# Feed-forward gate and up products of a two-layer trunk: eight half products against Strassen's seven

## The chip, the cores and the metric

One core of a Trainium2 chip runs the whole program. The metric is the device time of one execution in microseconds. Three runs of the kernel before gave 2757.32, 2754.48 and 2758.7 us, a median of 2757.32 us.

## The reference

A trunk of two layers works on 1088 tokens (1024 of a prompt and 64 of a running stream) of width 1024. Layer 0 mixes with a gated convolution and gated linear attention, layer 1 with banded softmax attention. Each layer ends with a SwiGLU feed-forward of inner width 2816:

```python
def swiglu_ffn(h, w_in, w_out):
    gate, up = jnp.split(h @ w_in, 2, axis=-1)
    return (jax.nn.silu(gate) * up) @ w_out
...
x = x + swiglu_ffn(rms_norm(x, norm_ffn[layer]), w_ffn_in[layer], w_ffn_out[layer])
```

Everything is float32, and the results are wanted at about that precision.

## The kernel before

Activations lie transposed: the 1024 features are 8 tiles of 128 partitions (`KT`), the 1088 tokens are the free axis, cut into groups of 384, 384 and 320 (`GROUPS`). To keep precision, each operand is split into a rounded part "hi" and a rest "lo", and each product is three matmuls: hi·hi, hi·lo and lo·hi. The split is a cast on ScalarE (ACT) and a subtraction on VectorE (DVE). `chain` (L241) is one output tile for one token group: 3 matmuls for each of the tiles of the inner axis into one PSUM bank, then an evacuation. `gemm` (L253) is three chains with one weight tile, so 72 matmuls for 8 inner tiles.

Weights come in one list in order of use. `fetch` (L219) issues the DMA of the next one from the queue of SyncE (SP) into the only raw buffer `wraw` and splits it into one of two buffers `whi` and `wlo`. `next_weights` (L236) hands out one weight tile and fetches another, so that one split tile and one on its way are ahead of the matmuls. TensorE (PE) runs in the order of the program text; the order of the other engines and of the SP queue is set by a list scheduler that takes what is ready first by its own model, with priorities; instructions within an engine's queue, once placed, start in that order. `order` (L41) is a planner that spreads side work (norms, attention units) between the matmuls.

The feed-forward (`ffn`, L720) walks the 22 inner tiles in three parts (8, 7 and 7, `FPARTS` L27). For each inner tile it runs a gate gemm and an up gemm over all 8 feature tiles (L740, L741). The gate evacuation multiplies by the reciprocal norm `RS` (L730) and applies SiLU on ACT; the up evacuation multiplies by `RS` (L736), by the gate (L737) and splits the result (L271). After each part `out_gemm` (L716) multiplies the part's tiles with the second weight matrix, eight output tiles, and adds each chain to the residual `X` (L705), which lies in SBUF for the whole feed-forward. In the last part of layer 0 the evacuation also makes the next layer's split input (L266, L267), its sum of squares (POOL, L279) and a store to DRAM (L758); in layer 1 it stores the result (L1164).

The output projection ahead of the feed-forward of layer 1 (L1156 to L1163) starts with 18 short chains of two inner tiles.

Of the kernel before, what the change touches and what calls it, by code (L numbers as in the profile page):

```python
# [131 lines left out]
def trunk_kernel(  # L132
# [6 lines left out]
    act, dve, pe, sp = nc.scalar, nc.vector, nc.tensor, nc.sync  # L139
    order = PEOrder()  # L140
# [6 lines left out]
    apool = ctx.enter_context(tc.tile_pool(name="apool", bufs=1))  # L147
# [17 lines left out]
    RS = [const.tile([P, c1 - c0], F32, name=f"rs{i}") for i, (c0, c1) in enumerate(GROUPS)]  # L165
# [24 lines left out]
    def mm_tile():  # L190
        return cur["ps"].tile([P, 512], F32, name="mm")

    def mm(out, lhsT, rhs, start, stop):
        pe.matmul(out, lhsT, rhs, start=start, stop=stop)  # L194
        n = rhs.free_size()
        order.spend(max(214.0, n / 0.6) if lhsT.dtype == F32 else max(107.0, n / 2.4))
# [3 lines left out]
        order.spend(107.0)  # L200


    wlist = [(w_in[i], KT) for i in range(w_in.shape[0])] + [(w_out[n], KT) for n in range(KT)]
    def ffn_weights(layer):
        for f0, f1 in FPARTS:
            for f in range(f0, f1):
                wlist.append((w_f1[layer, 2 * f], KT))
                wlist.append((w_f1[layer, 2 * f + 1], KT))
# [10 lines left out]
    def fetch():  # L219
        if wpos[0] == len(wlist):  # L220
            return
        src, nk = wlist[wpos[0]]
        wpos[0] += 1
        raw = wpool.tile([P, KT, P], F32, name="wraw", bufs=1)
        sp.dma_start(raw[:, 0:nk, :], src)
# [8 lines left out]
        wready.append((hi, lo))  # L234
# [27 lines left out]
    def scratch():  # L262
        return scratch_r().bitcast(F32)
# [286 lines left out]
    e = dd[1]  # L550
# [169 lines left out]
    def ffn(layer, xgn, aslots, X, after, nxt, g_idx):  # L720
        for pi, (f0, f1) in enumerate(FPARTS):
            acts = []
            for f in range(f0, f1):
                ah, al = aslots[f - f0]
                acts.append((ah, al))
                sbuf_s = {}

                def evac_gate(g, c0, c1, ps):
                    s = scratch()[:, 0:c1 - c0]
                    dve.tensor_tensor(s, ps, RS[g], op=ALU.mult)  # L730
                    silu(s)
                    sbuf_s[g] = s

                def evac_up(g, c0, c1, ps):
                    u = tmp.tile([P, GW], F32, name="ta")[:, 0:c1 - c0]
                    dve.tensor_tensor(u, ps, RS[g], op=ALU.mult)  # L736
                    dve.tensor_tensor(u, u, sbuf_s[g], op=ALU.mult)  # L737
                    split(u, ah[:, c0:c1], al[:, c0:c1])

                gemm(xgn, evac_gate)  # L740
                gemm(xgn, evac_up)  # L741
            last = pi == len(FPARTS) - 1
            if last and nxt is not None:
                log_exp_tables()
            out_gemm(acts, X, after, nxt, last, g_idx)


    mx0.close()
    f0 = ctx.enter_context(ExitStack())
    cur["ps"] = f0.enter_context(tc.tile_pool(name="ps1", bufs=6, space=PSUM))  # L750
    x_sp = dram.tile([KT, P, T], F32, name="x_sp")
    a_sp = dram.tile([KT, P, T], F32, name="a_sp")
    with tc.tile_pool(name="xres", bufs=1, side="right") as xp:
# [398 lines left out]
    X = [bp.tile([P, T], F32, name=f"x1_{n}") for n in range(KT)]
    for g, (c0, c1) in enumerate(GROUPS):
        for n in range(KT):
            sp.dma_start(X[n][:, c0:c1], x_sp[n, :, c0:c1])
    wb = [next_weights() for _ in range(w_ob.shape[0])]  # L1156
    for g in range(len(GROUPS)):
        for n in range(NA):
            ks = slice(n % NB * (KT - KA), (n % NB + 1) * (KT - KA))
            hi, lo = wb[n // NB]  # L1160
            chain((hi[:, ks, :], lo[:, ks, :]), Y1[KA:], g, out_evac(X, n, None, xgf, True, 3))
    for n in range(NA, KT):
        gemm(Y1, out_evac(X, n, None, xgf, True, 3))  # L1163
    ffn(1, xgf, Y1, X, lambda n, c0, c1: sp.dma_start(o_y[n, :, c0:c1], X[n][:, c0:c1]), None, 0)  # L1164
    order.flush()


# [87 lines left out]
```

## Time and profile before

| what | us |
|---|---|
| median of 3 runs | 2757.32 |
| the profiled execution | 2754.32 |
| its span, first to last instruction | 2752.6 |
| PE busy (matmul) in the span | 2683.9 |
| DVE busy | 1309.3 |
| ACT busy | 972.2 |
| POOL busy | 294.8 |

The granted clock of PE is 0.995 of full speed over the span. The two feed-forwards lie at about 483 to 1271 us and 1965 to 2752 us; the attention of layer 1 lies between them, and the mixers of layer 0 ahead. Rows of the profile name an engine, a source line, an operation, the output and the inputs with their shapes, then a count and durations. A duration of a single matmul row overlaps with the next: the pace of PE is the distance from start to start. SPq rows are issues of DMAs by SP.

### The profile page before, as it was taken

To read this page: it belongs to the slowest core of one execution; us is meant where nothing else is said; L and a number is where in the kernel's file an instruction comes from. 1 tells how busy PE (TensorE), PEld (TensorE's weight loads), DVE (VectorE), ACT (ScalarE), POOL (GpSimd) and SP (SyncE) were. 2 spreads that over 40 slices of the span, in tenths; PEclk is the share of its full clock that TensorE was granted. 3 is DMA by queue.
4 is the path that set the end of the run, shared out by engine and by line. 5 is a ranking of instruction groups with operands and counts; after the bars stand their busy time and mean duration, and the time that the engine had idled before them with its cause. 6 is when DMAs were issued, how large, how long until landed. Compare 5 with 4: busy or idle time off the path is not lost.

```text
span 2752.6 us, 40413 instructions
## 1 busy us (share of the span) xinstructions
PE 2683.9 (98%) x16514; PEld 2619.9 (95%) x16514; DVE 1309.3 (48%) x2797; ACT 972.2 (35%) x1950; POOL 294.8 (11%) x361
## 2 busy tenths in 40 slices
PE   8999999999999999999999999989999999999999
PEld 8888999999999999999888888979999999999999
DVE  7545444433233323344778777775633223323332
ACT  5524123321012112234777778865422112211210
POOL 0000002000000000013333333342200000000000
PEclk9999999999999999999999999999999999999999
DMA  5010131111111111122111111143211111111112
GB/s 170 24 34 27 46 105 53 39 47 46 46 47 39 45 48 47 45 79 93 49 57 56 53 55 52 55 136 128 74 39 47 46 46 47 39 47 47 47 54 82
DMA packets 73738, 160.75 MB, mean 58 GB/s; under 512 B 11296, under 2 KB 44592, under 8 KB 73520
## 3 DMA queue, kind: packets, MB, share of 16 engines
q1 hardware_dynamic: 73552, 158.16, 17.9%
q8 instruction: 130, 2.13, 0.3%
q14 instruction: 56, 0.46, 0.1%
HBM read 136.98 MB, written 25.08 MB: 59 GB/s over the span
## 4 chain that ended last, share of the span: by engine, by line
PE 81%; ACT 8%; DVE 7%; issue 2%; DMA 2%; POOL 1%; SPq 0%; DVEq 0%; POOLq 0%; ACTq 0%
PE mm L194 75%; ACT s L932 2%; DVE s L928 1%; PE ao L194 1%; PE pt L199 1%; PE misc L194 1%; PE kv L194 1%; ACT ph L270 1%; ACT s L936 1%; DVE pl L271 1%; PE S L194 1%; ACT whi L229 1%; PE tr L194 1%; DVE s L938 1%; DMA ta<-in_cv_dram 1%
## 5 line engine op out<-in xcount | busy, mean ns | idle before, releaser
L194 PE MATMUL mm<-a,whi 128*128 128x384 f32 (+1 forms) x5760 | 1453.6, 332 | 10.5 <-DVE x L705 5.1
L194 PEld LDWEIGHTS mm<-a,whi 128*128 128x128 f32 x5760 | 1021.0, 189 | 24.2 <-DVE x L705 7.6
L194 PE MATMUL mm<-a,wlo 128*128 128x384 f32 (+1 forms) x2880 | 951.0, 330 | 0.0
L194 PEld LDWEIGHTS mm<-a,wlo 128*128 128x128 f32 x2880 | 543.5, 189 | 5.1 <-issue 1.2
L229 ACT CAST whi<-wraw 128x1024 fp32r<-128x1024 f32 (+2 forms) x201 | 205.7, 1023 | 633.4 <-PE mm L194 624.7
L194 PE MATMUL mm<-bh,wlo 128*128 128x384 f32 (+1 forms) x1056 | 344.7, 326 | 0.0
L194 PE MATMUL mm<-bh,whi 128*128 128x384 f32 (+1 forms) x1056 | 344.4, 326 | 0.0
L194 PE MATMUL mm<-bl,whi 128*128 128x384 f32 (+1 forms) x1056 | 344.2, 326 | 0.0
L730 DVE TENSOR_TENSOR ts<-mm,rs 128x384 f32<-128x384 f32 x132 | 70.7, 535 | 348.9 <-PE mm L194 348.9
L231 DVE TENSOR_TENSOR wlo<-wraw,whi 128x1024 fp32r<-128x1024 f32 (+1 forms) x171 | 205.1, 1200 | 52.3 <-ACT whi L229 52.3
L194 PEld LDWEIGHTS mm<-bh,whi 128*128 128x128 f32 x1056 | 198.2, 188 | 0.2
L194 PEld LDWEIGHTS mm<-bl,whi 128*128 128x128 f32 x1056 | 198.2, 188 | 0.1
L194 PEld LDWEIGHTS mm<-bh,wlo 128*128 128x128 f32 x1056 | 198.2, 188 | 0.1
L279 POOL TENSOR_TENSOR rs<-rs,ta 128x384 f32<-128x384 f32 (+1 forms) x54 | 58.3, 1079 | 1241.6 <-ACT ta L278 1241.0
L736 DVE TENSOR_TENSOR ta<-mm,rs 128x384 f32<-128x384 f32 x132 | 70.7, 536 | 224.7 <-PE mm L194 224.7
L186 ACT ACTIVATE ts<-ts 128x384 f32<-128x384 f32 (+1 forms) x130 | 65.7, 505 | 294.4 <-DVE ts L730 294.4
L705 DVE TENSOR_TENSOR x<-x,mm 128x384 f32<-128x384 f32 (+1 forms) x96 | 50.6, 530 | 199.1 <-PE mm L194 192.2
L705 DVE TENSOR_TENSOR xr<-xr,mm 128x384 f32<-128x384 f32 (+1 forms) x96 | 51.1, 532 | 195.4 <-PE mm L194 195.4
L932 ACT ACTIVATE s<-s,mx 128x640 f32<-128x640 f32 (+4 forms) x144 | 101.6, 705 | 64.3 <-DVE mx L928 63.3
L199 PE MATMUL pt<-ident,s 128*128 128x128 f32 x560 | 93.0, 277 | 16.9 <-DVE pl L271 8.5
L271 DVE TENSOR_TENSOR pl<-pt,ph 128x384 fp32r<-128x384 f32 (+2 forms) x192 | 90.4, 486 | 34.7 <-ACT ph L270 33.6
L270 ACT CAST a<-ta 128x384 fp32r<-128x384 f32 (+1 forms) x72 | 35.6, 496 | 173.6 <-DVE ta L737 170.1
(258 smaller groups left out, 3693.6 us busy)
## 6 DMA issues: line engine op xcount, KB each, us to landing
wraw<-in_w_f_dram SPq DMA_DIRECT2D x104, 512.0 KB, 3.2
wraw<-in_w_f_dram SPq DMA_DIRECT2D x32, 448.0 KB, 3.3
wraw<-in_w_qkv_dram SPq DMA_DIRECT2D x24, 512.0 KB, 3.5
wraw<-in_w_in_dram SPq DMA_DIRECT2D x23, 512.0 KB, 3.5
B<-in_bias_dram SPq DMA_DIRECT2D x16, 320.0 KB, 2.9
xr<-in_xT_dram SPq DMA_DIRECT2D x8, 544.0 KB, 6.8
wraw<-in_w_out_dram SPq DMA_DIRECT2D x8, 512.0 KB, 3.5
a_sp<-ao SPq DMA_DIRECT2D x28, 128.0 KB, 1.7
```

The lines of the kernel that those rows point to most:

```text
L186: cur["silu"] = act.activation(x, x, AF.Silu).ins
L194: pe.matmul(out, lhsT, rhs, start=start, stop=stop)
L199: pe.transpose(out, in_, idn)
L229: act.copy(hi[:, 0:nk, :], raw[:, 0:nk, :])
L231: cur["sub"].tensor_tensor(lo[:, a:b, :], raw[:, a:b, :], hi[:, a:b, :].bitcast(F32), op=ALU.subtract)
L270: act.copy(hi, x)
L271: sub.tensor_tensor(lo, x, hi.bitcast(F32), op=ALU.subtract)
L279: add.tensor_tensor(RS[g], RS[g], sq[:, 0:n], op=ALU.add)
L705: dve.tensor_tensor(xv, xv, ps, op=ALU.add)
L730: dve.tensor_tensor(s, ps, RS[g], op=ALU.mult)
L736: dve.tensor_tensor(u, ps, RS[g], op=ALU.mult)
L932: act.activation(s[rows, 0:nk], s[rows, 0:nk], AF.Exp, bias=mx[rows, 0:1], scale=-1.0, accum_out=mx[rows, 1:2])
```

## The change

For 20 of the 22 inner tiles, taken in pairs, the gate (and the up) products of token groups 0 and 1 are computed by Strassen's scheme in its form with seven products: the weights of two inner tiles, halved along the feature axis, are the 2 by 2 blocks of one operand, the two token groups halved along the features those of the other. Each of the seven products has 4 feature tiles. The block sums of the activations (`T1`, `T2`, `T4`, `T3`) are made once for each layer during the first part, from the residual in DRAM, times gain and `RS`; those of the weights are made for each pair in `fetch_pair`. Group 2 is computed as before, with the unsummed weights. The first part has the 2 inner tiles that are not paired, then come five parts of 4.

The residual no longer stays in SBUF: each output tile of each part is loaded from `x_sp` in DRAM, added to, and stored again. The stages ahead of the feed-forward store it there. PSUM has 8 banks for these stages, where it had 6. `next_weights` fetches only when no weight is ready, and one step ahead for the first pair.

```diff
-FPARTS = [(0, 8), (8, 15), (15, 22)]
+FPARTS = [(0, 2), (2, 6), (6, 10), (10, 14), (14, 18), (18, 22)]
+KH = 4
...
+    def fetch_pair(raw1, src1, src2):
+        fw = cur["fw"]
+        raw2 = fw.tile([P, KT, P], F32, name="wraw2", bufs=1)
+        sp.dma_start(raw1, src1)
+        sp.dma_start(raw2, src2)
+        w1 = split_weights(raw1, KT)
+        a11, a12 = raw1[:, 0:KH, :], raw1[:, KH:KT, :]
+        a21, a22 = raw2[:, 0:KH, :], raw2[:, KH:KT, :]
+        es = [(fw.tile([P, KT, P], F32R, name="shi"), fw.tile([P, KT, P], F32R, name="slo")) for _ in range(2)]
+        def put(e, half, r):
+            hi, lo = [t[:, half * KH:(half + 1) * KH, :] for t in es[e]]
+            act.copy(hi, r)
+            dve.tensor_tensor(lo, r, hi.bitcast(F32), op=ALU.subtract)
+        def summed(a, b, op):
+            r = fw.tile([P, KH, P], F32, name="sraw")
+            dve.tensor_tensor(r, a, b, op=op)
+            return r
+        with tc.high_priority(offset=-100):
+            s1 = summed(a21, a22, ALU.add)
+            s2 = summed(s1, a11, ALU.subtract)
+            put(0, 0, s2)
+            put(1, 0, s1)
+            dve.tensor_tensor(a11, a11, a21, op=ALU.subtract)
+            put(0, 1, a11)
+            dve.tensor_tensor(s2, a12, s2, op=ALU.subtract)
+            put(1, 1, s2)
+        return w1, split_weights(raw2, KT), es[0], es[1]
 
     def next_weights():
         w = wready.pop(0)
-        fetch()
+        if not wready:
+            fetch()
+        if wpos[0] < len(wlist) and not isinstance(wlist[wpos[0]][1], int) and isinstance(wlist[wpos[0] - 1][1], int):
+            fetch()
         return w
...
+            def operands():
+                for k in range(KH):
+                    early.append(fw.tile([P, KT * P], F32, name=("shi", "slo")[k % 2]))
+                    for t, c0, c1 in ((early[k], a0, a1), (late[k], b0, b1)):
+                        sp.dma_start(t[:, 0:GW], x_sp[k, :, c0:c1])
+                        sp.dma_start(t[:, GW:2 * GW], x_sp[k + KH, :, c0:c1])
+                for k in range(KH):
+                    b11, b21 = early[k][:, 0:GW], early[k][:, GW:2 * GW]
+                    b12, b22 = late[k][:, 0:GW], late[k][:, GW:2 * GW]
+                    for v, kk, g in ((b11, k, 0), (b12, k, 1), (b22, k + KH, 1), (b21, k + KH, 0)):
+                        dve.scalar_tensor_tensor(v, v, gain[:, g_in, kk:kk + 1], RS[g], op0=ALU.mult, op1=ALU.mult)
+                    t1 = tmp.tile([P, GW], F32, name="ta")
+                    dve.tensor_tensor(t1, b12, b11, op=ALU.subtract)
+                    split(t1, *T1[k])
+                    t2 = tmp.tile([P, GW], F32, name="ta")
+                    dve.tensor_tensor(t2, b22, t1, op=ALU.subtract)
+                    split(t2, *T2[k])
+                    t4 = tmp.tile([P, GW], F32, name="ta")
+                    dve.tensor_tensor(t4, t2, b21, op=ALU.subtract)
+                    split(t4, *T4[k])
+                    dve.tensor_tensor(b12, b22, b12, op=ALU.subtract)
+                    yield 7000.0
+            def operands_late(k):
+                split(early[k][:, 0:GW], *B11[k])
+                split(early[k][:, GW:2 * GW], *B21[k])
+                split(late[k][:, 0:GW], *T3[k])
+                split(late[k][:, GW:2 * GW], *B22[k])
+            def fast(make):
+                w1, w2, w23, w14 = next_weights()
+                def seven(w, half, acts):
+                    ps = mm_tile()[:, 0:GW]
+                    product(ps, rows_of(w, half), acts, True, True)
+                    return ps
+                p1 = seven(w1, 0, B11)
+                s1 = scratch()
+                act.copy(s1, p1)
+                pe1 = mm_tile()[:, 0:e1 - e0]
+                product(pe1, rows_of(w1, 0), G2[0], True, False)
+                p6 = seven(w23, 0, T2)
+                u2 = scratch()
+                dve.tensor_tensor(u2, s1, p6, op=ALU.add)
+                p2 = seven(w1, 1, B21)
+                make(0, 0, s1, ALU.add, p2)
+                product(pe1, rows_of(w1, 1), G2[1], False, True)
+                make(0, 2, RS[2], ALU.mult, pe1)
+                p7 = seven(w23, 1, T3)
+                u3 = scratch()
+                dve.tensor_tensor(u3, u2, p7, op=ALU.add)
+                p5 = seven(w14, 0, T1)
+                make(1, 1, u3, ALU.add, p5)
+                dve.tensor_tensor(u2, u2, p5, op=ALU.add)
+                p4 = seven(w2, 1, T4)
+                make(1, 0, u3, ALU.subtract, p4)
+                pe2 = mm_tile()[:, 0:e1 - e0]
+                product(pe2, rows_of(w2, 1), G2[1], True, False)
+                product(pe2, rows_of(w2, 0), G2[0], False, True)
+                make(1, 2, RS[2], ALU.mult, pe2)
+                p3 = seven(w14, 1, B22)
+                make(0, 1, u2, ALU.add, p3)
...
+                        def gate(i, g, t, op, ps):
+                            c0, c1 = GROUPS[g]
+                            s = sg[i][:, c0:c1]
+                            dve.tensor_tensor(s, t, ps, op=op)
+                            silu(s)
+                        def up(i, g, t, op, ps):
+                            c0, c1 = GROUPS[g]
+                            s = sg[i][:, c0:c1]
+                            u = tmp.tile([P, GW], F32, name="ta")[:, 0:c1 - c0]
+                            dve.tensor_tensor(u, t, ps, op=op)
+                            dve.tensor_tensor(s, u, s, op=ALU.mult)
+                            split(s, *[t[:, c0:c1] for t in acts[j + i]])
+                        fast(gate)
+                        fast(up)
...
+                def residual(n):
+                    x = wide()
+                    sp.dma_start(x, x_sp[n])
+                    return x
+                x_next = residual(0)
+                for n in range(KT):
+                    if pi == 0 and n < KH:
+                        operands_late(n)
+                    x, x_next = x_next, residual(n + 1) if n + 1 < KT else None
+                    evac = out_evac([x] * KT, n, lambda n, c0, c1: sp.dma_start((dst if last else x_sp)[n, :, c0:c1], x[:, c0:c1]),
+                                    nxt if last else None, True, g_out)
+                    w = next_weights()
+                    for g in (0, 2, 1) if n == 0 else (0, 1, 2):
+                        chain(w, acts, g, evac)
```

`wide()` hands out one of two buffers of 1088 columns (`sg`), used in turn for the gates of a pair and for the residual. `early` and `late` use buffers that are free in the first part (those of the weight sums, and of the inner tiles 2 and 3).

## Rows read from the trace of the kernel before

**Rows 1.** The page's first part: busy time, share of the span, instructions of each engine.

```profile
PE 2683.9 (98%) x16514; PEld 2619.9 (95%) x16514; DVE 1309.3 (48%) x2797; ACT 972.2 (35%) x1950; POOL 294.8 (11%) x361
```

**Rows 2.** Windows in the two feed-forwards: stretch, length, each engine's busy time, clock, DMA.

```profile
480.00:660.00 180.00, 180.00 (x1089) 179.31 (x1088) 70.62 (x117) 44.39 (x73) 0.00 (x0) 1.00 0.13 45
2450.00:2600.00 150.00, 150.00 (x912) 150.00 (x911) 49.51 (x78) 25.04 (x38) 0.00 (x0) 1.00 0.15 48
```

**Rows 3.** Timeline, pace of matmuls of 384 and 320 columns: start, duration, instruction.

```profile
1181.52 0.51 PE L194 MATMUL mm<-a,whi 128*128 128x384 f32 x2
...
1182.04 0.51 PE L194 MATMUL mm<-a,whi 128*128 128x384 f32 x2
...
1184.99 0.46 PE L194 MATMUL mm<-a,whi 128*128 128x320 f32 x2
...
1185.43 0.46 PE L194 MATMUL mm<-a,whi 128*128 128x320 f32 x2
```

**Rows 4.** Groups by line and shape: busy us, mean ns, then idle time ahead.

```profile
L231 DVE TENSOR_TENSOR wlo<-wraw,whi 128x1024 fp32r<-128x1024 f32 x139 | 170.2, 1225 | 42.4 <-ACT whi L229 42.4
L229 ACT CAST whi<-wraw 128x1024 fp32r<-128x1024 f32 x161 | 168.8, 1048 | 438.0 <-PE mm L194 430.7 <-DMA wraw<-in_w_in_dram 5.3 <-DMA wraw<-in_w_out_dram 1.8
L231 DVE TENSOR_TENSOR wlo<-wraw,whi 128x896 fp32r<-128x896 f32 x32 | 34.9, 1092 | 9.9 <-ACT whi L229 9.9
L229 ACT CAST whi<-wraw 128x896 fp32r<-128x896 f32 x32 | 30.2, 944 | 191.4 <-PE mm L194 190.0 <-issue 1.4
L737 DVE TENSOR_TENSOR ta<-ta,ts 128x384 f32<-128x384 f32 x88 | 49.1, 558 | 3.1
L730 DVE TENSOR_TENSOR ts<-mm,rs 128x320 f32<-128x320 f32 x44 | 21.6, 492 | 129.1 <-PE mm L194 129.1
L271 DVE TENSOR_TENSOR a<-ta,a 128x384 fp32r<-128x384 f32 x46 | 25.7, 558 | 25.8 <-ACT a L270 25.8
L267 DVE SCALAR_TENSOR_TENSOR a<-xr,gain,a 128x384 fp32r<-128x384 f32 x32 | 19.8, 619 | 22.0 <-ACT a L266 22.0
```

**Rows 5.** DMA issues, sizes and median us to landing; then the eight residual loads' spread.

```profile
wraw<-in_w_f_dram SPq DMA_DIRECT2D x104, 512.0 KB, 3.2
...
x_sp<-xr SPq DMA_DIRECT2D x16, 192.0 KB, 1.9
...
ta<-in_ckT_dram SPq DMA_DIRECT2D x16, 128.0 KB, 2.1
...
DMA to landing us min/median/max: 3.8/6.8/10.4
```

**Rows 6.** Windows with the DMA engines full: last columns are DMA share and GB/s.

```profile
1919.00:1931.00 12.00, 10.39 (x57) 9.03 (x55) 9.57 (x17) 7.94 (x16) 6.12 (x6) 1.00 1.04 368
395.00:406.00 11.00, 11.00 (x69) 11.00 (x68) 3.38 (x6) 2.99 (x6) 0.00 (x0) 1.00 0.99 397
```

**Rows 7.** Timeline, one weight split in a feed-forward; then SP's longest wait.

```profile
713.26 1.05 ACT L229 CAST whi<-wraw 128x1024 fp32r<-128x1024 f32 x1 [10.81 <-PE mm L194]
...
714.35 1.23 DVE L231 TENSOR_TENSOR wlo<-wraw,whi 128x1024 fp32r<-128x1024 f32 x1 [0.45 <-ACT whi L229]
...
SPq L225 <- DVE wlo L231: 1305.5, 167, 28.1
```

**Rows 8.** Windows and one wait in the short chains ahead of layer 1's feed-forward.

```profile
1935.00:1940.00 5.00, 2.02 (x11) 1.75 (x11) 5.00 (x9) 1.91 (x6) 2.83 (x3) 0.91 0.35 105
1940.00:1945.00 5.00, 5.00 (x24) 5.00 (x23) 5.00 (x7) 4.48 (x10) 3.35 (x4) 0.75 0.26 78
...
PEld mm L194 <- DVE x L705: 5.0, 4, 3.2
```

**Rows 9.** Timeline, evacuation of the last up chain of a part.

```profile
1187.48 0.31 PE L194 MATMUL mm<-a,wlo 128*128 128x320 f32 x1
...
1187.83 0.49 DVE L736 TENSOR_TENSOR ta<-mm,rs 128x320 f32<-128x320 f32 x1 [1.22 <-PE mm L194]
...
1189.76 0.49 DVE L271 TENSOR_TENSOR ya1l<-ta,ya1h 128x320 fp32r<-128x320 f32 x1
```

More of the change, by code (lines that the diff above doesn't have):

```diff
@@ L146, in trunk_kernel @@
     tmp = ctx.enter_context(tc.tile_pool(name="tmp", bufs=2))
[L147 removed]
+    a0x = ctx.enter_context(ExitStack())
+    apool = a0x.enter_context(tc.tile_pool(name="apool", bufs=1))
     dram = ctx.enter_context(tc.tile_pool(name="dram", bufs=1, space=DRAM))
@@ L204, in ffn_weights @@
     def ffn_weights(layer):
[L205 to L208, printed above, removed]
+        for pi, (f0, f1) in enumerate(FPARTS):
+            if pi == 0:
+                wlist.extend((w_f1[layer, 2 * f + s], KT) for f in range(f0, f1) for s in range(2))
+            else:
+                wlist.extend((w_f1[layer, 2 * f + s], w_f1[layer, 2 * f + 2 + s])
+                             for f in range(f0, f1, 2) for s in range(2))
             for n in range(KT):
@@ L217, in trunk_kernel, with split_weights @@
     wpos = [0]
[L219 to L225, printed above, removed]
+    def split_weights(raw, nk):
         hi = wpool.tile([P, KT, P], F32R, name="whi")
@@ L718, in out_gemm, with rows_of @@
             gemm(acts, out_evac(X, n, after, nxt, last, g_idx))
[L720 to L745, printed above, removed]
+    def rows_of(w, half):
+        return tuple(t[:, half * KH:(half + 1) * KH, :] for t in w)
@@ new lines, in product, with ffn, cut, slots @@
+    def product(ps, w, acts, first, last):
+        hi, lo = w
+        for k, (ah, al) in enumerate(acts):
+            mm(ps, hi[:, k, :], ah, first and k == 0, False)
+            mm(ps, hi[:, k, :], al, False, False)
+            mm(ps, lo[:, k, :], ah, False, last and k == len(acts) - 1)
+    def ffn(layer, xgn, g_in, dst, nxt, g_out):
+        (a0, a1), (b0, b1), (e0, e1) = GROUPS
+        with ExitStack() as fx:
+            tp = fx.enter_context(tc.tile_pool(name="ft", bufs=1))
+            hp = fx.enter_context(tc.tile_pool(name="fh", bufs=1))
+            fw = fx.enter_context(tc.tile_pool(name="fw", bufs=2))
+            cur["fw"] = fw
+            T1, T2, T4 = [[tuple(tp.tile([P, GW], F32R, name=f"t{j}{q}{k}") for q in "hl") for k in range(KH)]
+                          for j in (1, 2, 4)]
+            def cut(k, c0, c1):
+                return xgn[k][0][:, c0:c1], xgn[k][1][:, c0:c1]
+            lo_k, hi_k = range(KH), range(KH, KT)
+            B11, B21 = [cut(k, a0, a1) for k in lo_k], [cut(k, a0, a1) for k in hi_k]
+            T3, B22 = [cut(k, b0, b1) for k in lo_k], [cut(k, b0, b1) for k in hi_k]
+            G2 = [[cut(k, e0, e1) for k in ks] for ks in (lo_k, hi_k)]
+            def slots(n):
+                return [tuple(hp.tile([P, T], F32R, name=f"h{q}{i}") for q in "hl") for i in range(n)]
+            def wide():
+                return fw.tile([P, T], F32, name="sg")
+            late = [hp.tile([P, T], F32, name=f"h{q}{i}") for i in (2, 3) for q in "hl"]
+            early = []
+            def operands():
[57 more added lines that the diff above has]
+                make(0, 1, u2, ALU.add, p3)
+            for pi, (f0, f1) in enumerate(FPARTS):
+                acts = slots(f1 - f0)
+                if pi == 0:
+                    order.start(operands(), 9000.0)
+                    for ah, al in acts:
+                        sbuf_s = {}
+                        def evac_gate(g, c0, c1, ps):
+                            s = scratch()[:, 0:c1 - c0]
+                            dve.tensor_tensor(s, ps, RS[g], op=ALU.mult)
+                            silu(s)
+                            sbuf_s[g] = s
+                        def evac_up(g, c0, c1, ps):
+                            u = tmp.tile([P, GW], F32, name="ta")[:, 0:c1 - c0]
+                            dve.tensor_tensor(u, ps, RS[g], op=ALU.mult)
+                            dve.tensor_tensor(u, u, sbuf_s[g], op=ALU.mult)
+                            split(u, ah[:, c0:c1], al[:, c0:c1])
+                        gemm(xgn, evac_gate)
+                        gemm(xgn, evac_up)
+                else:
+                    for j in range(0, f1 - f0, 2):
+                        sg = [wide(), wide()]
+                        def gate(i, g, t, op, ps):
+                            c0, c1 = GROUPS[g]
+                            s = sg[i][:, c0:c1]
+                            dve.tensor_tensor(s, t, ps, op=op)
+                            silu(s)
+                        def up(i, g, t, op, ps):
+                            c0, c1 = GROUPS[g]
+                            s = sg[i][:, c0:c1]
+                            u = tmp.tile([P, GW], F32, name="ta")[:, 0:c1 - c0]
+                            dve.tensor_tensor(u, t, ps, op=op)
[3 more added lines that the diff above has]
+                        fast(up)
+                last = pi == len(FPARTS) - 1
+                if last and nxt is not None:
+                    log_exp_tables()
+                def residual(n):
[12 more added lines that the diff above has]
+                        chain(w, acts, g, evac)
+            order.flush()
@@ L756, in trunk_kernel @@
             sp.dma_start(X[n], xT[:, n, :])
-        out_gemm(YB + YA, X, None, xg, True, 1)
-        ffn(0, xg, YB + YA, X, lambda n, c0, c1: sp.dma_start(x_sp[n, :, c0:c1], X[n][:, c0:c1]), xg, 2)
-        order.flush()
+        out_gemm(YB + YA, X, spill(X), xg, True, 1)
     l0.close()
+    ffn(0, xg, 1, x_sp, xg, 2)
     f0.close()
@@ L1147, in trunk_kernel @@
         cur["sub"] = dve
-    cur["ps"] = ctx.enter_context(tc.tile_pool(name="ps3", bufs=6, space=PSUM))
+    cur["ps"] = ctx.enter_context(tc.tile_pool(name="ps3", bufs=8, space=PSUM))
     bp = ctx.enter_context(tc.tile_pool(name="bpool", bufs=1, side="right"))
     xgf = pair_tiles(bp, "b", KT)
[L1152 to L1165, printed above, removed]
+    with tc.tile_pool(name="x1", bufs=1, side="right") as xp:
+        X = [xp.tile([P, T], F32, name=f"x1_{n}") for n in range(KT)]
+        for g, (c0, c1) in enumerate(GROUPS):
+            for n in range(KT):
+                sp.dma_start(X[n][:, c0:c1], x_sp[n, :, c0:c1])
+        wb = [next_weights() for _ in range(w_ob.shape[0])]
+        for g in range(len(GROUPS)):
+            for n in range(NA):
+                ks = slice(n % NB * (KT - KA), (n % NB + 1) * (KT - KA))
+                hi, lo = wb[n // NB]
+                chain((hi[:, ks, :], lo[:, ks, :]), Y1[KA:], g, out_evac(X, n, spill(X), xgf, True, 3))
+        for n in range(NA, KT):
+            gemm(Y1, out_evac(X, n, spill(X), xgf, True, 3))
+    a0x.close()
+    ffn(1, xgf, 3, o_y, None, 0)
 def kernel(**inputs):
```

17 lines of the change are left out of this document (15 added, 2 removed).

## The prediction

> **What bounds the kernel now.** I read the busy totals first: PE works 2683.9 of 2752.6 us, every other engine less than half [rows 1]. Then windows inside the two feed-forwards, where the whole change lies: PE is busy all of them, at full clock, with 1089 matmuls in 180 us and 912 in 150; DVE works 33 to 39% and the DMA engines 13 to 15% [rows 2]. The pace comes from starts in the timeline: three matmuls of 384 columns take 0.52 us, 173 ns each; three of 320 take 0.44, 147 ns each [rows 3]. So these stages are bound by the number of matmuls alone, and one gemm of 72 takes 48 × 0.173 + 24 × 0.147 = 11.85 us. The weight stream explains how this stays dense: the cast starts just after the gemm that held its buffer, having sat idle 10.81 us for PE, the subtraction ends 2.3 us later, and SP spends 1305 us waiting for it to free the raw buffer [rows 7]. There are some 9 us of slack in each gemm of 11.85.
>
> **What is removed.** One call of `fast` replaces two gemms. For groups 0 and 1 these have 2 × 48 matmuls of 384 columns; seven products of 4 feature tiles times 3 have 84. Group 2 keeps its 48. So 12 matmuls × 0.173 = 2.08 us go for each call: 21.6 us instead of 23.7. Gate and up, 10 pairs, 2 layers make 40 calls: 480 matmuls, 83 us, all of it on PE's path.
>
> **What is added to DVE in a call.** A subtraction of 1024 columns is 1.225 us, of 896 1.092, hence 1.04 ns a column and about 0.69 us at 512 columns [rows 4]. A pair of weights needs 2 × 1.225 + 4 sums and 4 subtractions × 0.69 = 8.0 us, where two single tiles need 2.45. The evacuation has seven first operations at 0.557 and two at 0.492, 4.9 us; an up call has 12 more, 4 × 2 × 0.558 + 2 × 2 × 0.492 = 6.4 us. Gate 12.9, up 19.3; with 0.04 us between neighbours (50 instructions) 34.2 us for both, against 43.2 us of PE. 79% is heavy but fits; PE has 8 banks for the 9 results of a call, so an evacuation may be some 10 us late. The casts are lighter: on ACT 1.048 at 1024 columns, 0.944 at 896 [rows 4], so 0.63 at 512, and 2 × 1.05 + 4 × 0.63 = 4.6 us of weights plus seven short ones, some 8 of 21.6 us. The weight buffers come free in time: w1 is done 9.8 us into a call, the first sum 11.9, w2 19.5, the last sum 21.6, and their successors are first wanted at 0, 3.8, 13.9 and 11.9 us of the next call. The tightest is the first sum's second half and the last sum, with over 9 us for two casts and subtractions. Cost of the stage between 0 (cover holds) and 2 us a pair, 40 us (every subtraction waits out its cast, as in the 0.45 us of [rows 7]: 18 such waits × 0.5 bring DVE to 43 us, even with PE). I take 0.1 us a call, 4 us, near zero because the list scheduler has other ready work to put there.
>
> **Residual through DRAM, parts of 4.** A gemm of the second product now has 36 matmuls, 5.9 us. It loads 557 KB, stores as much and takes 262 KB of weights: 1.38 MB. The engines, full, move 368 to 397 GB/s [rows 6], so 3.6 us of 5.9. One residual buffer cycles through load (3.8 us alone, 6.8 in a crowd of eight), three additions (1.6) and the last store (1.9) [rows 4, 5]: 7.6 us, two buffers, so 3.8 us a tile. It fits, as does a weight (2.6 + 0.63 + 0.69 us plus a share of the queue). The change of part: g1 is put last in the first tile because the last product's evacuation takes some 2.4 us (from 1187.83 to 1190.25 in the like case [rows 9]); 3.8 us of other chains cover it. The first residual cannot load before the gates of the last call are used, so it lands some 4 us into the tile; eight banks hold that. SP's instructions that the next fetch is put behind in the program (two residual loads) could hold it up; the scheduler places what is ready first, and the fetch is ready some 10 us earlier, so I take 0. Three more parts add 72 residual additions a layer, covered. 0, with 43 us as the other end (a rival below).
>
> **The first part (2 tiles).** Here nothing fits well. Its second-product gemms have 18 matmuls, 2.96 us, and need 1.25 MB each: 3.2 us at full DMA speed. A weight's way is 2.1 us for 128 KB [rows 5], 0.42 for the cast, 0.43 for the subtraction and 0.3 of semaphores: 3.2 us, with the queue nearly full about 1 us more. DVE has 1.6 + 0.4 us, plus 4 subtractions of the late operands × 0.56 = 2.2 in the first four, so 4.2 us; and it comes in loaded, as the operand sums (per k four products by gain at 0.62, seven more operations at 0.56 [rows 4]: 6.4 us, 26 in all) lie beside 17 us of ordinary work in 47.4 us of PE. So a gemm takes between 3.2 and 5.0 us; I take 4.2: 8 × 1.24 × 2 layers = 20 us. The first chain waits for the last up evacuation, 2.4 us against one chain of 6 × 0.173: 1.5 × 2 = 3 us. The first pair's weights: 3.2 us for 512 KB [rows 5], a microsecond of queue, 2.3 for the split [rows 7], less the 2.96 us of the last gemm: 3.6, for two layers 7; bounds 0 and 12.
>
> **What waits do to the clock, and the banks.** In the short chains ahead of layer 1's feed-forward DVE is busy without a gap, PE only 2.02 of 5 us, and then the granted clock is 0.91 and 0.75 in two stretches [rows 8], between the levels of 2.4 and 1.2 GHz. The 0.09 and 0.25 that are missing are 1.7 us of 10. The first part's waits look alike: 2 us a layer, 4 in all, between 0 and the 27 of a rival below. In that same stage two more banks let PE run two chains of 1.04 us further ahead of DVE, which it waits for 5.0 us there: 2 us gained (0 to 2). The 48 new stores of the residual there and in layer 0 go out behind additions already made; stores of this kind run in the last part of layer 0 now; nothing.
>
> **Sum.** −83 + 4 + 20 + 3 + 7 + 4 − 2 = −47 us. The profiled execution took 2754.3 us (span 2752.6 and 1.7 around it), so 2707; the median of the runs shown is 3.0 us above that execution: 2710 us.
>
> **Rivals.**
> 1. The first part costs little (weights at 3.2 us a gemm, no clock loss): −83 + 4 + 4 + 2 + 2 − 2, so −73: 2684. For it: PE's eight banks absorb late residuals. Against: loads, stores and weights share a full queue.
> 2. DVE becomes the bound of the calls: 2 us a pair more, +36 over my 4: 2746. For it: an up call has 19.3 of 21.6 us on DVE. Against: gate and up average out, and the weights may be prepared a call ahead.
> 3. Half clock through the first part's second product: each gemm then 5.9 instead of 4.2 us, 1.7 × 16 = 27, less the 4 counted: 2733. For it: [rows 8]. Against: that fall followed a stretch in which PE stood for 3 of 5 us; the waits here are about 1.2 us each. The Trainium skill (TensorE: Matmul & The Clock Gate, "HAM oscillation — how this bites in real kernels") has the array fall back when bursts of matmuls alternate with waits for DMA, burst after burst; by that rule this rival holds. The trace before has only one such fall in the stages concerned, to 0.75 over 5 us.
> 4. SP's queue holds the weight for the second tile of each part of 4: issued behind two residual loads that wait for the last gate (2.7 us after the part begins), it lands after 2.7 + 0.5 + 2.9 + 2.6 us, is split 1.5 later at 10.2, wanted at 5.9: 4.3 × 10 parts = 43: 2753, no change. Against: the scheduler's order by readiness.
> 5. Slower: the two residual buffers set the pace of all parts of 4. If a load takes 10.4 us as the last of eight did [rows 5], a cycle is 13.9 us and a tile 7.0 instead of 5.9: 1.1 × 80 tiles = 88 us, 2798. The sign turns where a tile takes 6.5 us, a landing of 9.5 us. Against: 60% load on the DMA engines, two loads in flight at most.
>
> **Chances.** Forecast 0.53, rivals 0.17, 0.10, 0.06, 0.07, 0.07. The likeliest case alone spans 2693 to 2728. From the bounds: low 2678 (rival 1 with the calls at no cost), high 2752 (rivals 2 and 3 inside, 4 half, 5 outside); about 0.13 is left out. A measurement tells 0.2%, some 5.5 us, from no change. Faster 0.87 (forecast, rivals 1 to 3 and a little of 4), same 0.04, slower 0.09.
>
> **What would show it.** PE with 480 matmuls fewer, and windows in the calls busy throughout with 132 matmuls in 21.6 us: the gain. In the first part's second product (some 24 us of work, at about 530 and 2015 us) waits of PE's weight load for `wlo`, 35 us instead of 24. DVE between 70 and 85% in the calls. Gaps at the second tile of every part would mean rival 4; gaps before chains for a bank, released by L705's like, rival 5; DVE without idle time and PE waiting for it in an up call, rival 2. The forecast is wrong if PE has over 60 us of gaps in the two feed-forwards, or under 15.

## The result and the profile after

The changed kernel takes 2717.77 us (median of 4 runs, 2716.0 to 2722.08) where the kernel before took 2755.9 on the same chip: 0.9863 of it, 95% interval 0.9846 to 0.988, some 38 us less. The forecast was 2710, the range 2678 to 2752. The profiled execution took 2719.06 us, its span 2717.2.

The page's first part, as in [rows 1]: PE has 480 instructions fewer, DVE works 377 us more.

```profile
PE 2621.9 (96%) x16034; PEld 2550.1 (94%) x16034; DVE 1685.9 (62%) x3549; ACT 1118.1 (41%) x2254; POOL 297.0 (11%) x361
```

PE's idle time rose from 68.7 us to 95.3, so something of the gain was given back. Windows of 620 us over the five parts of 4 in either layer, as in [rows 2], show that it was not there. A window's columns are the stretch and its length, the busy time of PE, of PE's weight loads, of DVE, ACT and POOL, each with its instructions, the granted clock, the DMA share and GB/s:

```profile
590.00:1210.00 620.00, 620.00 (x3773) 620.00 (x3772) 361.76 (x621) 175.45 (x296) 3.26 (x3) 1.00 0.35 108
2060.00:2680.00 620.00, 620.00 (x3774) 620.00 (x3774) 357.88 (x614) 168.50 (x283) 0.00 (x0) 1.00 0.35 109
```

PE has no gap, at 164 ns a matmul, the mean pace of [rows 3] (two of 173 and one of 147). The four calls of the first part of 4 one by one, then its second product:

```profile
573.00:594.60 21.60, 21.60 (x130) 21.60 (x130) 15.53 (x25) 8.45 (x15) 0.00 (x0) 0.98 0.29 93
594.60:616.20 21.60, 21.60 (x134) 21.60 (x133) 16.02 (x29) 7.75 (x14) 0.00 (x0) 1.00 0.15 49
616.20:637.80 21.60, 21.60 (x134) 21.60 (x133) 13.53 (x23) 7.79 (x14) 0.00 (x0) 1.00 0.13 37
637.80:659.40 21.60, 21.60 (x133) 21.60 (x133) 12.05 (x24) 4.68 (x10) 0.00 (x0) 1.00 0.14 42
659.40:706.90 47.50, 47.50 (x290) 47.50 (x289) 23.21 (x41) 8.45 (x13) 0.00 (x0) 1.00 0.71 227
```

A call is 132 matmuls in 21.6 us, as forecast; DVE works 15.5 and 16.0 us in the first gate and up call and 13.5 and 12.1 in the next two. The second product moves 227 GB/s beside PE and costs PE nothing. The losses lie in three other places. Windows of 10 us: four in the first part's second product of layer 0, four in that of layer 1, two at the end of layer 0:

```profile
540.00:550.00 10.00, 9.31 (x54) 8.46 (x52) 2.79 (x7) 0.81 (x2) 0.00 (x0) 1.00 0.77 220
550.00:560.00 10.00, 6.64 (x28) 5.92 (x29) 3.44 (x8) 0.81 (x2) 0.00 (x0) 0.83 0.74 222
560.00:570.00 10.00, 5.39 (x30) 4.37 (x28) 4.79 (x9) 2.32 (x4) 0.00 (x0) 1.00 0.85 259
570.00:580.00 10.00, 9.56 (x48) 9.56 (x49) 7.21 (x13) 2.82 (x6) 0.00 (x0) 0.83 0.63 215
...
2010.00:2020.00 10.00, 8.64 (x50) 7.87 (x49) 2.68 (x7) 0.81 (x2) 0.00 (x0) 1.00 0.74 230
2020.00:2030.00 10.00, 6.98 (x28) 6.98 (x29) 3.09 (x8) 0.81 (x2) 0.00 (x0) 0.66 0.59 171
2030.00:2040.00 10.00, 6.34 (x28) 5.51 (x26) 3.95 (x8) 1.13 (x2) 0.00 (x0) 0.83 0.83 255
2040.00:2050.00 10.00, 8.99 (x43) 8.67 (x44) 7.82 (x12) 4.01 (x7) 0.00 (x0) 0.83 0.65 211
...
1240.00:1250.00 10.00, 5.69 (x24) 3.52 (x22) 8.39 (x15) 6.94 (x15) 4.97 (x8) 0.82 0.42 146
1250.00:1260.00 10.00, 8.46 (x35) 8.46 (x36) 3.05 (x10) 1.45 (x3) 0.62 (x2) 0.67 0.20 80
```

In such windows I count two losses: length less PE's busy time, and length times the share of the clock that is missing. The second is a little too large, as a low clock costs nothing while PE stands, as from 2021 to 2023 us. Over the stages this gives, in us:

| stage | before: idle, clock | after: idle, clock | change |
|---|---|---|---|
| mixers and projection of layer 0 | 19.4, 5.2 | 16.9, 3.4 | −4.3 |
| first part and its second product, layer 0 | 0, 0 | 11.0, 3.4 | +14.4 |
| parts of 4, layer 0 | 0, 0 | 0, 0 | 0 |
| end of layer 0 | 1.8, 0 | 5.8, 5.1 | +9.1 |
| attention | 38.7, 5.1 | 41.8, 11.9 | +9.9 |
| out projection and start of layer 1's feed-forward | 5.4, 1.8 | 5.3, 1.7 | −0.2 |
| first part and its second product, layer 1 | 0, 0 | 11.0, 6.8 | +17.8 |
| rest | 3.3, 0.6 | 3.3, 0 | −0.6 |

Together +46; 83 less 46 is 37, and the spans differ by 35.4. In layer 0's first part the waits view names the weights: who waits, for whom, us in total, times, longest. Then one of these waits, the ACT timeline there, casts of 256 columns, and SP's issues of two of these weights, each behind a load of the residual (`sg<-x_sp`):

```profile
PE mm L196 <- ACT whi L228: 8.3, 5, 3.1
...
551.97 0.44 PE L196 MATMUL mm<-hh,whi 128*128 128x384 f32 x1 [2.21 <-ACT whi L228]
...
545.60 0.40 ACT L228 CAST whi<-wraw 128x256 fp32r<-128x256 f32 x1 [3.73 <-DMA wraw<-in_w_f_dram]
551.51 0.40 ACT L228 CAST whi<-wraw 128x256 fp32r<-128x256 f32 x1 [5.51 <-DMA wraw<-in_w_f_dram]
557.64 0.40 ACT L228 CAST whi<-wraw 128x256 fp32r<-128x256 f32 x1 [5.72 <-DMA wraw<-in_w_f_dram]
...
545.30 0.32 SPq L923 DMA_DIRECT2D sg<-x_sp  x1
...
547.20 0.44 SPq L244 DMA_DIRECT2D wraw<-in_w_f_dram  x1
...
551.24 0.38 SPq L923 DMA_DIRECT2D sg<-x_sp  x1
...
552.40 0.33 SPq L244 DMA_DIRECT2D wraw<-in_w_f_dram  x1
```

The cast stands for its transfer each time: issued at 547.2, cast at 551.5; issued at 552.4, cast at 557.6. Six such issues lie 3.4 to 6.1 us apart, 4.7 in the mean; a gemm of PE there is 2.96 us. The first two, with no load of the residual just ahead of them, were cast 2.3 and 2.5 us after their issue, the four behind such a load 3.2 to 5.2 us after it. SP issues the next weight within 0.4 us of the subtraction that frees the buffer. The issues view gives the landing of these 128 KB, and of the residual:

```profile
sg<-x_sp SPq DMA_DIRECT2D x96, 544.0 KB, 4.1
...
x_sp<-sg SPq DMA_DIRECT2D x176, 192.0 KB, 2.5
...
wraw<-in_w_f_dram SPq DMA_DIRECT2D x16, 128.0 KB, 2.7
```

At the end of layer 0 the PE timeline has the three norm matmuls and the attention's first ones:

```profile
1242.54 0.81 PE L196 MATMUL mm<-rs,ones 128*128 128x384 f32 x2
1244.57 0.91 PE L196 MATMUL mm<-rs,ones 128*128 128x384 f32 x2 [1.22 <-DVE rs L327]
1247.96 1.43 PE L196 MATMUL mm<-rs,ones 128*128 128x320 f32 x2 [2.48 <-DVE rs L327]
1251.54 1.01 PE L196 MATMUL mm<-a,whi 128*128 128x384 f32 x2 [2.15 <-DVE ts L334]
```

They wait for DVE's sums of squares: the last output tile now takes 5.9 us on PE, not 10.4, and DVE, whose instructions for it took 6.7 us, is still at it. Before there was one wait here, of 1.82 us:

```profile
1273.94 0.81 PE L194 MATMUL mm<-rs,ones 128*128 128x320 f32 x2 [1.82 <-DVE rs L279]
```

DVE's timeline, of the multiplications by gain of 320 columns and the last sum, and then POOL's:

```profile
1232.31 0.54 DVE L315 SCALAR_TENSOR_TENSOR a<-sg,gain,a 128x320 fp32r<-128x320 f32 x1
...
1238.88 1.17 DVE L315 SCALAR_TENSOR_TENSOR a<-sg,gain,a 128x320 fp32r<-128x320 f32 x1
...
1245.24 1.19 DVE L315 SCALAR_TENSOR_TENSOR a<-sg,gain,a 128x320 fp32r<-128x320 f32 x1 [0.73 <-ACT a L314]
1246.36 1.55 DVE L327 TENSOR_TENSOR rs<-rs,ta 128x320 f32<-128x320 f32 x1
```

```profile
1238.61 1.09 POOL L327 TENSOR_TENSOR rs<-rs,ta 128x320 f32<-128x320 f32 x1 [0.82 <-ACT ta L326]
1244.82 2.74 POOL L230 TENSOR_TENSOR wlo<-wraw,whi 128x512 fp32r<-128x512 f32 x2 [5.12 <-ACT whi L228]
```

The same multiplication takes 0.54 us, and 1.17 to 1.19 where it begins inside an operation of POOL; the last sum, for which PE waits, begins in one too and takes 1.55 us, where a sum of 384 columns just before took 0.55. By these rows the last multiplication and the last sum came some 1.7 us late, which is an estimate. Moving POOL's two weight subtractions was not tried.

### The profile page after: what moved, and what is told of

Read it like the earlier page. It is cut to its first block, busy times and chain, and to the rows that moved or that the text cites. A ratio compares the mean times of both kernels' runs of the same rounds, so it can differ in the third digit from the quotient of the medians.

```text
span 2717.2 us, 41649 instructions
## 1 busy us (share of the span) xinstructions
PE 2621.9 (96%) x16034; PEld 2550.1 (94%) x16034; DVE 1685.9 (62%) x3549; ACT 1118.1 (41%) x2254; POOL 297.0 (11%) x361
## 4 chain that ended last, share of the span: by engine, by line
PE 76%; DVE 9%; ACT 8%; DMA 4%; issue 2%; POOL 1%; SPq 0%; DVEq 0%; ACTq 0%; POOLq 0%
PE mm L196 70%; ACT s L1126 1%; PE ao L196 1%; DVE s L1122 1%; PE pt L201 1%; PE misc L196 1%; PE kv L196 1%; DMA wraw<-in_w_f_dram 1%; ACT ph L318 1%; PE S L196 1%; ACT whi L228 1%; DMA ta<-in_cv_dram 1%; DVE pl L319 1%; DMA x_sp<-sg 1%; ACT s L1130 1%
## 5 line engine op out<-in xcount | busy, mean ns | idle before, releaser
L196 PE MATMUL mm<-a,whi 128*128 128x384 f32 (+1 forms) x3744 | 956.7, 333 | 12.5 <-ACT whi L228 5.1
L196 PEld LDWEIGHTS mm<-a,whi 128*128 128x128 f32 x3744 | 665.7, 190 | 26.6 <-ACT whi L228 5.9
L196 PE MATMUL mm<-a,wlo 128*128 128x384 f32 (+1 forms) x1872 | 620.9, 332 | 4.5 <-DVE wlo L230 4.5
L228 ACT CAST whi<-wraw 128x1024 fp32r<-128x1024 f32 (+3 forms) x249 | 214.6, 863 | 481.6 <-PE mm L196 406.4
L196 PE MATMUL mm<-hh,whi 128*128 128x384 f32 (+1 forms) x1056 | 347.3, 329 | 13.5 <-ACT whi L228 11.4
L196 PE MATMUL mm<-hh,wlo 128*128 128x384 f32 (+1 forms) x1056 | 347.8, 329 | 0.3 <-DVE wlo L230 0.2
L196 PE MATMUL mm<-hl,whi 128*128 128x384 f32 (+1 forms) x1056 | 346.8, 328 | 0.6 <-DVE hl L319 0.6
L230 DVE TENSOR_TENSOR wlo<-wraw,whi 128x1024 fp32r<-128x1024 f32 (+3 forms) x219 | 214.8, 981 | 46.4 <-ACT whi L228 44.0
L196 PEld LDWEIGHTS mm<-hh,whi 128*128 128x128 f32 x1056 | 199.9, 189 | 15.9 <-ACT whi L228 13.3
L196 PEld LDWEIGHTS mm<-hh,wlo 128*128 128x128 f32 x1056 | 199.9, 189 | 1.6 <-DVE wlo L230 1.6
L201 PE MATMUL pt<-ident,s 128*128 128x128 f32 x560 | 94.1, 279 | 19.3 <-DVE pl L319 14.4
## 6 DMA issues: line engine op xcount, KB each, us to landing
sg<-x_sp SPq DMA_DIRECT2D x96, 544.0 KB, 4.1
```

Source lines behind the costliest of these rows:

```text
L201: pe.transpose(out, in_, idn)
```

## The experiments

e1 to e5 and e10 are edits of the changed kernel; e6 to e9 build on e1. "Before" is the kernel before, run beside them on the same chip. "By windows" means the two losses of the table, added.

**e1, second weights of the first part in two transfers.**

```diff
-            for n in range(KT):
-                wlist.append((w_f2[layer, n, :, f0:f1, :], f1 - f0))
+            if pi == 0:
+                for n in (0, 4):
+                    wlist.append((w_f2[layer, n:n + 4, :, f0:f1, :].rearrange("n p f c -> p n f c"), 4 * (f1 - f0)))
+            else:
+                for n in range(KT):
+                    wlist.append((w_f2[layer, n, :, f0:f1, :], f1 - f0))
...
```

> The second weights of the first part (2 tiles) come in two transfers of four output tiles each instead of eight, so they are split before the part's second product begins; nothing else changes. Theory (the weight's way, 128 KB transfer then cast then subtraction, sets the pace there): PE's idle and half-clock time in that stage, now 14.4 us in layer 0 and 17.8 in layer 1, falls to about 4 each, 2696 us. Rival (the full DMA queue and the two residual buffers set it): at least 12 each remain, 2710 us or more.

Measured: 2699.3 us, 0.9792 of before (0.9777 to 0.9807), 18 us below the changed kernel. The waits for the cast are gone from that stage. What PE still waits for at 525 to 580 us is the residual's addition:

```profile
PE mm L196 <- DVE sg L760: 4.1, 2, 2.7
PE mm L196 <- ACT hh L325: 0.8, 1, 0.8
PE mm L196 <- DVE hl L326: 0.4, 1, 0.4
```

The weight's way set the pace; the residual's round trip stood behind it. By windows the stage lost 7.0 us in layer 0 and 12.5 in layer 1, not the 4 each of the theory: 12.7 of the 18 us came back there. Another 5 lie in the attention, which this edit does not touch.

**e2, no flush at the end of layer 0.**

```diff
-            order.flush()
+            if nxt is None:
+                order.flush()
```

> Layer 0's feed-forward no longer flushes the planner at its end, so the three norm matmuls are placed among the matmuls of the attention's first projection and not directly behind the last chains. Theory (PE stands for DVE, which is late because the last part's output tiles are 5.9 us and not 10.4): the 10 us of idle and half clock around 1240 to 1260 us shrink to 3 or 4, 2711 us. Rival (the norm is wanted at once anyway, with two PSUM banks in the attention): 2716 to 2720 us.

Measured: 2716.53 us, 0.9857 (0.9842 to 0.9872): no gain. The rival held. The waits of PE at 1235 to 1265 us are now for the projection's evacuation, which waits for the norm and keeps a bank:

```profile
PE mm L196 <- DVE qr L975: 4.2, 1, 4.2
```

**e3, ordinary products in the new layout.**

```diff
-            if pi == 0:
-                wlist.extend((w_f1[layer, 2 * f + s], KT) for f in range(f0, f1) for s in range(2))
-            else:
-                wlist.extend((w_f1[layer, 2 * f + s], w_f1[layer, 2 * f + 2 + s])
-                             for f in range(f0, f1, 2) for s in range(2))
+            wlist.extend((w_f1[layer, 2 * f + s], KT) for f in range(f0, f1) for s in range(2))
...
-                    order.start(operands(), 9000.0)
...
-                if pi == 0:
+                if True:
                     for ah, al in acts:
...
-                    if pi == 0 and n < KH:
-                        operands_late(n)
```

> Parts of 2 and 4 tiles, the residual in DRAM and eight banks stay; the gate and up products are all the ordinary ones, without operand sums and weight pairs. Theory (the seven products give all of 83 us, and the new layout costs some 35 by itself): 2717.8 + 83 less about 8 for the operand work in the first part, 2790 us. Rival (the seven products give much less than 83, and the layout costs little): below 2770 us.

Measured: 2793.22 us (2 runs), 1.0133 of before (1.0113 to 1.0153). PE is dense in the parts of 4 here too:

```profile
590.00:1250.00 660.00, 660.00 (x4008) 660.00 (x4007) 250.96 (x416) 126.48 (x205) 4.31 (x4) 1.00 0.32 101
```

So the layout by itself costs 37 us, and the seven products with all that they need bring 75 (2793.2 less 2717.8). Of the 83 on PE 8 are missing: the first part loses 24 us in both layers here and 32 in the changed kernel, by windows; 3 of the difference are idle time and 5 clock. The layout's cost lies, by the same count, in the first part (24), at the end of layer 0 (8 more than before) and in the attention (7 more); the mixers lose 4 less. The end of layer 0 and most of the attention's loss thus come with ordinary products too.

**e4, six banks.**

```diff
-    cur["ps"] = f0.enter_context(tc.tile_pool(name="ps1", bufs=8, space=PSUM))
+    cur["ps"] = f0.enter_context(tc.tile_pool(name="ps1", bufs=6, space=PSUM))
...
-    cur["ps"] = ctx.enter_context(tc.tile_pool(name="ps3", bufs=8, space=PSUM))
+    cur["ps"] = ctx.enter_context(tc.tile_pool(name="ps3", bufs=6, space=PSUM))
```

> Six PSUM banks for the feed-forward stages, as before the change, instead of eight. Theory (DVE takes a result within 2 or 3 us in the calls, so the nine results need no more than six banks; in the second products of the parts of 4 the first residual lands about 4 us in): 2718 to 2724 us, PE dense from 590 to 1210 us. Rival (the two banks are what hides DVE's extra work and the residual): 2730 us or more, gaps in every call or at every part.

Measured: 2717.48 us, 0.9855 (0.9839 to 0.9872), the same, and PE as dense:

```profile
590.00:1210.00 620.00, 620.00 (x3772) 620.00 (x3771) 360.73 (x620) 175.26 (x296) 3.13 (x3) 1.00 0.34 109
```

The two banks hide nothing that six don't.

**e5, DVE's weight sums twice.**

```diff
             act.copy(hi, r)
-            dve.tensor_tensor(lo, r, hi.bitcast(F32), op=ALU.subtract)
+            for _ in range(2):
+                dve.tensor_tensor(lo, r, hi.bitcast(F32), op=ALU.subtract)
...
-            dve.tensor_tensor(r, a, b, op=op)
+            for _ in range(2):
+                dve.tensor_tensor(r, a, b, op=op)
```

> The changed kernel with the DVE work of the weight pairs done twice: each sum of 512 columns and each subtraction behind a cast of a sum is issued two times, 6 instructions of about 0.69 us or 4.1 us more in each of the 40 calls. Theory (DVE has a third of a call to spare and eight banks cover its lateness): DVE rises from 66% to some 84% of a call, PE stays dense from 590 to 1210 us, and the time rises by the first part alone, 2718 to 2724 us. Rival (DVE is near its bound in the calls): 2740 us or more.

Measured: 2719.39 us (2 runs), 0.986 (0.984 to 0.988): no change. Two calls, the first two of the four shown above, and the long window:

```profile
573.00:594.60 21.60, 21.60 (x131) 21.60 (x130) 20.04 (x33) 8.41 (x14) 0.00 (x0) 0.98 0.28 93
594.60:616.20 21.60, 21.60 (x134) 21.60 (x133) 19.14 (x34) 7.29 (x13) 0.00 (x0) 1.00 0.16 48
...
590.00:1210.00 620.00, 620.00 (x3773) 620.00 (x3772) 426.35 (x733) 173.91 (x296) 2.58 (x3) 1.00 0.35 109
```

DVE works 19 to 20 of 21.6 us and PE still has no gap. Rival 2 is out by a wide margin.

**e6, four more residual buffers in the first part, on e1.**

```diff
+                def residual(n, first=residual):
+                    if pi > 0 or n < KH:
+                        return first(n)
+                    sp.dma_start(late[n - KH], x_sp[n])
+                    return late[n - KH]
```

> On top of e1_group_w: in the first part the residuals of the last four output tiles are loaded into four buffers that the operand sums have left free, so that they need not wait for the two residual buffers. Theory (after e1 the second half of that stage waits for the residual's round trip, PE idle and half clock of some 4 us in layer 0 at 550 to 565 us and 5 in layer 1 at 2015 to 2030): these go, 2690 us. Rival (the full DMA queue sets it): 2696 us or more.

Measured: 2691.09 us, 0.9755 (0.9741 to 0.977), 8 us below e1. By windows the stage loses 2.3 us in layer 0 and 3.6 in layer 1, 13.6 less than in e1; attention and the end of layer 0 lose more here. The second half of layer 0's stage, where e1 had its waits for the addition, is dense, at 62 matmuls in 10 us:

```profile
545.00:555.00 10.00, 10.00 (x62) 9.85 (x61) 9.15 (x19) 2.19 (x3) 0.00 (x0) 1.00 0.70 221
555.00:565.00 10.00, 10.00 (x62) 10.00 (x61) 4.58 (x9) 1.52 (x2) 0.00 (x0) 1.00 0.80 294
```

**e7, late operand splits behind the last up evacuation, on e1.**

```diff
-                            split(u, ah[:, c0:c1], al[:, c0:c1])
+                            act.copy(ah[:, c0:c1], u)
+                            cur["up"] = dve.tensor_tensor(al[:, c0:c1], u, ah[:, c0:c1].bitcast(F32), op=ALU.subtract).ins
...
+                with tc.issue_after(cur["up"]):
```

> On top of e1_group_w: the late operand splits of the first part are placed on DVE behind the evacuation of the last up gemm; in e1 they lie between its instructions, and DVE works without a gap there. Theory (DVE holds the first second-product tile's input back, 1.2 us in layer 0, 4 us idle and 3 of half clock in layer 1 at 1990 to 2000 us): these mostly go, 2692 us. Rival (DVE has too much work in that part, and the wait only moves to the residual additions or the first pair's weights): 2697 to 2702 us.

Measured: 2705.17 us, 0.9807 (0.9791 to 0.9824), 6 us above e1. The wait at the stage's start fell to 0.7 us in either layer, but PE waits longer for the residual additions, 6.5 us at 525 to 585 (e1 had 4.1):

```profile
PE mm L196 <- DVE sg L760: 6.5, 5, 3.3
PE mm L196 <- DVE hl L902: 0.7, 1, 0.7
```

By windows the stage loses 8.9 us in layer 0 and 8.6 in layer 1, 17.5 together where e1 lost 19.5. So the edit gained 2 us where it works, less than the 7 expected, since the wait moved to the additions as the rival has it. The 6 us above e1 lie at the end of layer 0 (12.7 against 9.3) and in the attention (51.5 against 48.5); why is not shown.

**e8, other banks for the norm, on e1 and e2.**

```diff
-        ps = mm_tile()
+        ps = cur["bank"](g) if cur["bank"] else mm_tile()
...
+        cur["bank"] = lambda g: aps.tile([P, 512], F32, name=("ss", "misc", "S")[g], bufs=(1, 1, 2)[g])
         nxt = project(0)
+        cur["bank"] = None
```

> On top of e1_group_w and the missing flush of e2: the three norm matmuls at layer 0's end use PSUM banks of the attention's other tiles, not one of the two banks of its projections. Theory (in e2 PE stood for a bank that the projection's evacuation held while it waited for the norm; with the bank free PE goes on with the projection): the 10 us of idle and half clock at the end of layer 0 fall to 2 or 3, 2691 us. Rival (the projection cannot go on without the norm): 2697 to 2702 us.

Measured: 2695.02 us, 0.9771 (0.9757 to 0.9786). The interval overlaps that of e1. By windows, idle time and missing clock at the end of layer 0 are 5.4 us (1230 to 1250) where e1 had 9.3. These 3.9 us are about half of what was expected.

**e9, e1 with e6 and e8.** The edits are those above.

> The grouped weights of e1, the four further residual buffers of e6 and the norm banks of e8 together. Theory (they mend different waits): 2691 less the 4 us that e8 gained over e1, 2687 us, and PE without idle time between 530 and 600 us but for about a microsecond at the first tile. Rival (what e8 gained was within the scatter of the attention stage): 2690 to 2693 us.

Measured: 2686.37 us (5 runs, 2686.1 to 2687.88), 0.9744 of before (0.9731 to 0.9757): 31 us below the changed kernel, the fastest here, and as the theory has it. Windows at the end of layer 0 and in the first part's second product of layer 1:

```profile
1225.00:1235.00 10.00, 8.83 (x52) 8.34 (x51) 7.84 (x11) 5.12 (x11) 4.59 (x6) 1.00 0.49 163
1235.00:1245.00 10.00, 6.97 (x28) 5.96 (x27) 5.85 (x16) 5.24 (x11) 2.03 (x5) 0.86 0.35 120
...
1985.00:1995.00 10.00, 8.61 (x42) 8.33 (x43) 6.65 (x13) 0.99 (x3) 0.00 (x0) 0.83 0.79 261
1995.00:2005.00 10.00, 10.00 (x63) 10.00 (x62) 8.91 (x16) 2.90 (x5) 0.00 (x0) 1.00 0.72 234
2005.00:2015.00 10.00, 10.00 (x63) 10.00 (x62) 5.74 (x11) 1.53 (x2) 0.00 (x0) 1.00 0.90 309
```

**e10, the residual buffers alone.** The edit is that of e6, on the changed kernel.

> The changed kernel with the four further residual buffers of e6 in the first part and nothing else; the eight small weight transfers stay. Theory (the weight's way sets that stage's pace and the residual comes second, as e1 and e6 in this order say): at most 3 us gained, 2715 to 2718 us, with PE still waiting for the weights' cast. Rival (either of the two alone gives most of the 27 us of e1 and e6): 2708 us or less.

Measured: 2715.43 us, 0.9846 (0.9832 to 0.9859), 2 us, within what can be told from nothing. PE waits for the cast as before, at 525 to 585 us:

```profile
PE mm L196 <- ACT whi L228: 7.7, 5, 2.7
```

The two limits stand one behind the other: the residual shows only when the weights are out of the way.

## Why the prediction was right, and where its sizes were off

- **The gain of 83 us on PE** stands: 480 matmuls fewer, 21.6 us a call, no gap. The ordinary products in the same layout (e3) are 75 us slower; the 8 that are missing lie in the first part by windows (32 against 24). That the operand work there makes them is not shown.
- **The calls, 4 us taken, 0 to 40 as bounds:** 0. DVE's busy time in a part's first gate and up call, 31.6 us, is near the 32.2 of the sum; in the next two it is 25.6. So DVE was at 56 to 74% of a call, not at 70 to 85, and e5 shows that even 39 us of 43.2 would do. Rival 2 is refuted.
- **Parts of 4, residual through DRAM, 0 taken:** 0. The residual's loads of 557 KB (544.0 in the view's units) land in 4.1 us. The fetch behind two residual loads never held PE; rivals 4 and 5 do not occur.
- **The first part, 34 us with its clock (20 + 3 + 7 + 4):** 14.4 + 17.8 = 32.2. The mechanism was right: PE waits for the weights, though for the cast and not, as I had it, for `wlo`, and with them out of the way (e1) those waits are gone. The eight gemms lasted 33.6 us in layer 0 and 37.6 in layer 1, where 35 was forecast. Less the waits at the first tile (0.7 and 2.0 us) that is 4.3 us a gemm, clock included, where I took 4.2 and the clock beside it. The first pair's weights cost 3.7 and 2.7 us, near the 7. That the total fits so well is in part luck: the idle time was 22.0 us where 20 + 3 + 7 was taken, and the clock made up for it. A weight took 3.6 us from issue to cast in the mean, not the 3.1 of the sum, and the 0.3 us that the sum has for semaphores are shown by no row. The pace of 4.7 us did not hold for all eight gemms, because the first weights lay ready. Rival 1, 6 us for this stage, is out. The limit is the weight's way, not the number of residual buffers, as e10 shows; that the residual's loads slow the weights in the queue is what the timeline suggests, and no run separates the two.
- **Half clock (rival 3):** in part. Of the 32.2 us 10.2 are missing clock, where I took 4: the windows read 0.66 and 0.83 in places, full speed in others. Windows of 0.5 us show its two levels. It was at 1.2 GHz from 553.5 to 556.5 us, behind a wait of 2.21, and from 2021 to 2028, in and behind the longest, of 4.25. It stayed at 2.4 GHz behind waits of 1.39 and 1.33 us (557 to 563). The stage did not fall to half clock throughout, which would have been 27. In the example of the Trainium skill (TensorE: Matmul & The Clock Gate, "HAM oscillation — how this bites in real kernels") each burst of matmuls is shorter than the DMA wait behind it, and the clock is down in every burst; the prediction took over the alternation without that condition. Here a burst is 2.96 us, most waits were shorter, and the clock fell behind some of them only.
- **The two banks, −2:** 0. The stage ahead of layer 1's feed-forward lost 7.2 us before and 7.0 after, and six banks in the whole feed-forward (e4) change nothing.
- **The end of layer 0, not in the sum:** +9.1. This is the term that was missing. I gave shorter output tiles a cost on the DMA and the weights, but at the last tile three evacuations with gain, squares and norms follow in 5.9 us, and PE's next work is the norm itself. That shorter chains let DVE fall behind was to be seen in [rows 8]. e3 loses 9.7 us there with ordinary products, so the loss belongs to the new layout and not to the seven products. e8 gets back about half, by windows; how much of the rest is POOL's is open.
- **Attention and mixers, not touched:** +9.9 and −4.3. By the same count the ten experiments lose 48 to 53 us in the attention, 5 to 12 of it clock, though only e2, e8 and e9 touch it, at its start: kernels that differ elsewhere differ here by 5 us. So a difference of a few us between two experiments says nothing by itself; the windows of the edited stage must show it. All ten lie above the 43.8 of before, e3 with its ordinary products at 51, so some 5 to 7 us may belong to the layout and not to the products. The cause stays open, and that all 9.9 are a cost of the change is not shown.

Sum: −83 + 32 + 9 + 10 − 4 − 1 = −37 against −47.

## What to carry to other kernels

A stage that is cut into shorter pieces on the bounding engine must be priced by everything that comes once per piece: the transfer and split of its weight, the round trip of its buffer, and the evacuation of its last piece, each against the piece's new length. Where a small stage is paced by small transfers through a single buffer, fetch several pieces in one. Mend the limits in their order: here the second showed nothing until the first was gone.

## What the runs showed of the hardware

A load of 128 KB that took 2.1 us in the attention of the kernel before [rows 5], where the DMA engines were 18% busy, took 2.7 us in the median where they were 59 to 85% busy, and 3.2 to 5.2 us to its cast behind a load of the residual. DVE at 19 to 20 of 21.6 us in the first two calls of a part left PE without a gap, with eight banks; that load with six was not tried. PE's clock read 0.66 and 0.83 in windows where it stood for 3.0 to 3.7 of 10 us, 0.83 in two others where it stood for 0.4 and 1.0, and 1.00 from 560 to 570 us, where it stood for 4.6. A multiplication on DVE took 0.54 us, and 1.17 to 1.19 where it began inside an operation of POOL.
